# A two-layer attention trunk: hand-set order of the first stage, queued transposes, wider output chunks, last norm on VectorE

## Chip, core and metric

One NeuronCore of a Trainium2 chip runs the whole program in one launch. The metric is device time in microseconds (us), the median of several executions. PE is TensorE (PEld its weight loads), DVE is VectorE, ACT is ScalarE, POOL is GpSimd, and SP is the engine whose queue issues all DMAs here.

## What is computed

The input x is 512 tokens by 1024 features. Two layers follow each other, then one last RMSNorm. The four branches in a layer are latent attention (A), differential attention (B), top-k sparse attention (C) and a short convolution (D); each takes a slice of one input projection and is multiplied by a gate.

```
for l in range(2):
    h = rmsnorm(x, norm_g[l])
    p = split(h @ w_in[l])                 # 1024 -> 4040 columns
    o_a = mla(...); o_b = diff_attn(...); o_c = sparse(...); o_d = conv(...)
    y = concat([o_a * silu(gate_a), o_b * silu(gate_b), o_c * silu(gate_c), o_d * silu(gate_d)])
    x = x + y @ w_out[l]                   # 1024 x 1024
return rmsnorm(x, final_g)
```

## The kernel before

**Numbers.** Most products are made from float32 operands split into a high part and the rest, so that one product is three matmuls (`mm3`: high by high, high by rest, rest by high). A weight tile is loaded into a `wr` buffer (4 of them) and split by `split_w` (L103): ACT casts the high part `wh` (L106), POOL subtracts the rest `wl` in pieces of 256 columns (L101). `wh` and `wl` have 4 buffers each (`WB`).

**Order.** The program is written as streams that `merge` (L227) interleaves by estimated cost. A scheduler that works from a cost model then sets the order of each engine's queue. Inside `tc.manual_schedule(engines=...)` the engines named keep the order in which the program is written. Before the change only SP is named (`START`, L45), and only for the first stage of layer 0.

**First stage.** `FIRST[0]` (L30) is the list of its steps: `lT` loads token tile T of x (128 tokens), `wQ` loads a quarter Q of the first 456 weight columns, `sT` takes the squares and their sums on ACT (`Norm.part`), `nT` ends the norm (`Norm.finish`: Sqrt on ACT, five small DVE instructions, two DVE products with the norm weights g at L286), `eT` transposes the tile on PE (`Hidden.fill`, L302) and splits it (ACT cast L115, DVE subtraction L116), `cQ` splits a weight quarter (ACT cast, half of the subtraction on DVE at L108, half on POOL), and a pair of digits QT is the product of quarter Q with tile T (6 matmuls of 456 columns). After quarter 3 of a tile, `first_norm` (L521) works on that tile's result. `l0` also loads g, repeated to 128 rows, into a `wr` buffer (L245).

**Attention.** Six pairs of heads run per layer. A unit of a pair makes scores on PE, exponentials on ACT (L478) and normalised weights (L482). Two units later `turn` calls `flip` (L410), which transposes the 128x128 blocks of the weights on PE (L414), then casts (L115) and subtracts (L116). One unit later `prod` makes the product with the values (`ps_o`). 

**Output.** `out_first` (L859) multiplies the six parts of y that are ready early by w_out in four chunks of 256 columns: two weight tiles a chunk, four token tiles each, 18 matmuls per token tile. `LATE` (L47) puts the product of token tile 3 and chunk 3 off. `out_last` (L890) then adds the last two parts of y, 12 matmuls of 512 columns per token tile, and the matmuls put off. Each result is added to x on DVE (L888, L909) and handed to `after` (L1016), which makes the next norm: in layer 0 the squares, `finish` and, two token tiles later, the transposes of layer 1; in layer 1 the last norm, with `early` set: POOL multiplies by g in pieces of 256 columns (L272) while the squares are taken, and `finish` scales one half on DVE (L289) and one on ACT (L290).

Of the kernel before, what the change touches and what calls it, by code (L numbers as in the profile page):

```python
# [19 lines left out]
P = 128  # L20
# [9 lines left out]
FIRST = ("l0 w0 l1 l2 w1 l3 w2 w3 s0 n0 s1 c0 e0 00 n1 s2 c1 e1 01 10 11 n2 s3 e2 c2 02 12 20 21 n3 e3 c3 03 13 22 23 30 31 32 33",  # L30
# [14 lines left out]
START = {mybir.EngineType.SP}  # L45
FM = (456, 456)
LATE = ((3, 3),)  # L47
# [18 lines left out]
def hybrid_trunk(ctx, tc, x_in, norm_g, w_in, qa_g, w_uq, kva_g, w_ukv, dlam, subg,  # L66
# [55 lines left out]
    def mm3(o, terms, start=True, stop=True, skip=False):  # L122

        n = len(terms)
        for i, (ah, al, bh, bl) in enumerate(terms):
            for j, (a, b) in enumerate(((ah, bh), (ah, bl), (al, bh))):
                nc.tensor.matmul(o, lhsT=a, rhs=b, start=start and i == 0 and j == 0,  # L127
                                 stop=stop and i == n - 1 and j == 2, skip_group_check=skip)

# [118 lines left out]
    class Norm:  # L248


        def __init__(self, x, g, early=False):
            self.x, self.g, self.early = x, g, early
# [4 lines left out]
        def part(self, c):  # L257
            n, ss = self.n, self.ss
            self.n += 1
            jk = prob()  # L260
            nc.scalar.activation(jk[:, :c.stop - c.start], self.x[:, c], AF.Square, accum_out=ss[:, n:n + 1])
# [49 lines left out]
    def layer(l, hT, enter, after):  # L311
# [98 lines left out]
        def flip(p, qb, pts):  # L410
            nb = qb + 1
            b = bank("pt")
            for k in range(nb):
                nc.tensor.transpose(b[:, k * P:(k + 1) * P], p[:, k * P:(k + 1) * P], ident)  # L414
            c = (qb % 2) * P
            split_ps(pts[0][:, :nb, c:c + P], pts[1][:, :nb, c:c + P],
                     b[:, :nb * P].rearrange("p (k c) -> p k c", k=nb))
# [4 lines left out]
        def pair(k, unit, v, gt, post):  # L422

            yf = prob()
            for half in range(2):
                box = {}
                for j in range(2):
                    for qb in (2 * half, 2 * half + 1):
# [10 lines left out]
                        if qb % 2:  # L439
                            def prod(j=j, half=half, box=box):  # L440
# [4 lines left out]
                                pts = box[j]  # L445
                                for kb in range(nb):
# [3 lines left out]
                                        start=j == 0 and kb == 0, stop=j == 1 and kb == nb - 1, skip=True)  # L450
# [408 lines left out]
        def out_first():  # L859
# [7 lines left out]
            for n in range(4):  # L867
                c = slice(n * 256, (n + 1) * 256)
                ws = []
                for k0 in ((0, 3), (3, 6)):  # L870
                    raw = raw_tile()
                    rv = raw[:, :768].rearrange("p (k c) -> p k c", k=3)
                    if k0[0] == 0:
                        nc.sync.dma_start(rv, wo[:, 0:3, c])
                    else:
                        nc.sync.dma_start(rv[:, 0:1], wo[:, 3:4, c])
                        nc.sync.dma_start(rv[:, 1:3], wo[:, 6:8, c])
                    ws.append([w[:, :768].rearrange("p (k c) -> p k c", k=3) for w in split_w(raw, 768)])
                for t in range(NT):
                    ts_ = slice(t * P, (t + 1) * P)  # L880
                    terms = [(Y[k][:, 0, ts_], Y[k][:, 1, ts_], ws[i // 3][0][:, i % 3, :],
                              ws[i // 3][1][:, i % 3, :]) for i, k in enumerate(ks)]
# [4 lines left out]
                    yield from mm3g(o[:, :256], terms, 3, 0.33)  # L887
                    nc.vector.tensor_tensor(out=X[t][:, c], in0=o[:, :256], in1=X[t][:, c], op=OP.add)  # L888

        def out_last():  # L890
# [5 lines left out]
            for t in range(NT):  # L896
                ts_ = slice(t * P, (t + 1) * P)
                for n in range(2):
                    c = slice(n * 512, (n + 1) * 512)
                    o = bank("proj")  # L900
                    more = [m for m in (2 * n, 2 * n + 1) if (t, m) in put_off]
                    mm3(o, [(Y[4 + i][:, 0, ts_], Y[4 + i][:, 1, ts_], w[0][:, c], w[1][:, c])
                            for i, w in enumerate(ws)], stop=not more, skip=True)
                    for m in more:
                        mm3(o[:, (m % 2) * 256:(m % 2) * 256 + 256], put_off[t, m], start=False, stop=m == more[-1], skip=True)
# [85 lines left out]
    g0 = raw_tile()  # L991

    warm = sm.tile([P, 1], FT, name="warm", bufs=1)
    nc.scalar.activation(warm, ident[:, 0:1], AF.Sqrt)
# [99 lines left out]
```

## Time and profile before

| | us |
|---|---|
| median of 3 runs | 682.03 |
| lowest, highest | 677.0, 683.62 |
| profiled execution, its own time | 679.76 |
| its span in the trace | 678.0 |

The span is the time from the first to the last instruction on the core; 1.76 us of the execution lie outside it.

### The profile page before, as it was taken

To read this page: it belongs to the slowest core of one execution; us is meant where nothing else is said; L and a number is where in the kernel's file an instruction comes from. 1 tells how busy PE (TensorE), PEld (TensorE's weight loads), DVE (VectorE), ACT (ScalarE), POOL (GpSimd) and SP (SyncE) were. 2 spreads that over 40 slices of the span, in tenths; PEclk is the share of its full clock that TensorE was granted. 3 is DMA by queue.
4 is the path that set the end of the run, shared out by engine and by line. 5 is a ranking of instruction groups with operands and counts; after the bars stand their busy time and mean duration, and the time that the engine had idled before them with its cause. 6 is when DMAs were issued, how large, how long until landed. Compare 5 with 4: busy or idle time off the path is not lost.

```text
span 678.0 us, 11037 instructions
## 1 busy us (share of the span) xinstructions
PE 622.1 (92%) x3599; PEld 533.6 (79%) x3607; DVE 487.4 (72%) x1441; ACT 364.6 (54%) x879; POOL 278.5 (41%) x408
## 2 busy tenths in 40 slices
PE   1999999789999898999989899999999999999994
PEld 1877787678789677899968687879878977789994
DVE  3767762599999796645395767779999959664536
ACT  6556583484552564554364566866545256355435
POOL 2375432315434343442431854242534344344255
PEclk9999999799999999999999999999999999999998
DMA  8446573763455411233253653457244641132203
GB/s 262 117 111 191 148 133 94 185 158 99 109 145 151 118 47 43 83 125 114 58 169 91 181 171 103 139 135 170 65 115 116 190 117 48 47 109 100 80 1 125
DMA packets 86697, 80.71 MB, mean 119 GB/s; under 512 B 7302, under 2 KB 73400, under 8 KB 86640
## 3 DMA queue, kind: packets, MB, share of 16 engines
q1 hardware_dynamic: 86640, 80.02, 42.4%
q8 instruction: 28, 0.46, 0.3%
q14 instruction: 29, 0.24, 0.1%
HBM read 65.22 MB, written 12.16 MB: 114 GB/s over the span
## 4 chain that ended last, share of the span: by engine, by line
PE 58%; DVE 26%; ACT 7%; DMA 5%; issue 2%; POOL 1%; SPq 0%; ACTq 0%; DVEq 0%; POOLq 0%
PE ps_proj L127 43%; PE ps_o L127 5%; DVE ia L595 5%; DVE m L594 4%; PE ps_pt L414 3%; PE ps_s L127 2%; DMA wr<-in_w_in_dram 2%; DVE ptl L116 2%; DVE big L119 1%; DVE ps_s L490 1%; ACT prob L478 1%; DMA big<-in_x_dram 1%; PE ps_pt L302 1%; ACT prob L482 1%; DVE ia L581 1%
## 5 line engine op out<-in xcount | busy, mean ns | idle before, releaser
L101 POOL TENSOR_TENSOR wl<-wr,wh 128x256 fp32r<-128x256 f32 (+1 forms) x304 | 226.8, 779 | 326.1 <-ACT wh L106 279.4
L127 PE MATMUL ps_proj<-big,wh 128*128 128x512 f32 x768 | 250.7, 401 | 2.1 <-DVE prob L472 1.0
L127 PE MATMUL ps_proj<-wh,big 128*128 128x256 f32 (+2 forms) x768 | 173.1, 310 | 4.6 <-DVE big L116 2.1
L127 PEld LDWEIGHTS ps_proj<-big,wh 128*128 128x128 f32 x768 | 138.8, 189 | 26.8 <-issue 1.5
L127 PE MATMUL ps_proj<-big,wl 128*128 128x512 f32 x384 | 151.7, 395 | 0.0
L127 PEld LDWEIGHTS ps_proj<-wh,big 128*128 128x128 f32 x768 | 129.9, 193 | 9.6 <-DVE big L116 2.6
L127 PE MATMUL ps_proj<-wl,big 128*128 128x256 f32 (+2 forms) x384 | 116.8, 304 | 0.0
L106 ACT CAST wh<-wr 128x1024 fp32r<-128x1024 f32 (+2 forms) x84 | 83.8, 999 | 43.2 <-PE ps_proj L127 20.6
L127 PEld LDWEIGHTS ps_proj<-big,wl 128*128 128x128 f32 x384 | 72.3, 188 | 14.2
L127 PEld LDWEIGHTS ps_proj<-wl,big 128*128 128x128 f32 x384 | 74.4, 194 | 2.0
L116 DVE TENSOR_TENSOR ptl<-ps_pt,pth 128x128 fp32r<-128x128 f32 (+1 forms) x96 | 46.5, 485 | 31.4 <-ACT pth L115 30.8
L127 PE MATMUL ps_o<-pth,vt 128*128 128x256 f32 (+1 forms) x288 | 60.0, 280 | 5.2 <-ACT pth L115 3.9
L115 ACT CAST pth<-ps_pt 128x128 fp32r<-128x128 f32 (+1 forms) x96 | 40.5, 425 | 44.0 <-PE ps_pt L414 43.6
L478 ACT ACTIVATE prob<-ps_s,st_a 128x128 f32<-128x128 f32 (+1 forms) x64 | 33.8, 529 | 47.8 <-DVE st_a L490 30.7
L127 PEld LDWEIGHTS ps_o<-pth,vt 128*128 128x128 f32 x288 | 49.1, 194 | 10.0 <-ACT pth L115 6.5
L414 PE MATMUL ps_pt<-ident,prob 128*128 128x128 f32 x240 | 43.2, 278 | 10.2 <-ACT prob L482 7.1
L595 DVE MATCH_REPLACE8 ia<-m,ia 128x256 f32<-128x256 f32 (+2 forms) x96 | 52.0, 544 | 0.2
L594 DVE MAX8 m<-ia 128x8 f32<-128x256 f32 (+2 forms) x96 | 50.9, 550 | 0.1
L127 PE MATMUL ps_o<-ptl,vt 128*128 128x256 f32 (+1 forms) x144 | 42.3, 294 | 4.7 <-DVE ptl L116 4.7
L414 PEld LDWEIGHTS ps_pt<-ident,prob 128*128 128x128 f32 x240 | 28.5, 140 | 22.3 <-ACT prob L482 12.5
L482 ACT ACTIVATE prob<-prob,st_a 128x128 f32<-128x128 f32 (+1 forms) x64 | 35.8, 564 | 9.5 <-DVE st_a L481 9.3
L581 DVE SCALAR_TENSOR_TENSOR ia<-prob,widx,ia 128x256 f32<-128x256 f32 (+2 forms) x42 | 26.2, 639 | 12.7 <-ACT prob L576 12.0
(160 smaller groups left out, 949.1 us busy)
## 6 DMA issues: line engine op xcount, KB each, us to landing
wr<-in_w_in_dram SPq DMA_DIRECT2D x56, 512.0 KB
big<-trip SPq DMA_DIRECT2D x64, 128.0 KB
trip<-big SPq DMA_DIRECT2D x28, 256.0 KB
big<-in_x_dram SPq DMA_DIRECT2D x7, 512.0 KB
wr<-in_w_in_dram SPq DMA_DIRECT2D x8, 416.0 KB
big<-trip SPq DMA_DIRECT2D x32, 96.0 KB
wr<-in_w_out_dram SPq DMA_DIRECT2D x8, 384.0 KB
big<-big SPq DMA_DIRECT2D x8, 256.0 KB
```

Of the source, the lines that this page charges most:

```text
L101: nc.gpsimd.tensor_tensor(out=o[:, c], in0=a[:, c], in1=b[:, c], op=OP.subtract)
L106: nc.scalar.copy(h[:, :n], raw[:, :n])
L115: nc.scalar.copy(hi, src)
L116: nc.vector.tensor_tensor(out=lo, in0=src, in1=f(hi), op=OP.subtract)
L119: nc.vector.scalar_tensor_tensor(out=lo, in0=src, scalar=scale, in1=f(hi), op0=OP.mult, op1=OP.subtract)
L127: nc.tensor.matmul(o, lhsT=a, rhs=b, start=start and i == 0 and j == 0, stop=stop and i == n - 1 and j == 2, skip_group_check=skip)
L414: nc.tensor.transpose(b[:, k * P:(k + 1) * P], p[:, k * P:(k + 1) * P], ident)
L478: nc.scalar.activation(p[:, :W], s[:, :W], AF.Exp, scale=-1.0, bias=mn, accum_out=sums)
L482: nc.scalar.activation(p[:, :W], p[:, :W], AF.Copy, scale=st[:, 2:3])
L581: nc.vector.scalar_tensor_tensor(out=a, in0=r[:, :W], scalar=w, in1=a, op0=OP.mult, op1=OP.add)
L594: nc.vector.max(out=m8, in_=a)
L595: nc.vector.match_replace(out=a, in_to_replace=m8, in_values=a, imm_value=MARK)
```

## The change

Six things change.
1. START names ACT, DVE and PE beside SP, so in the first stage of layer 0 these keep the order of `FIRST[0]`, whose steps are rearranged.
2. g of layer 0 is loaded as one row of 4 KB and spread to 128 rows by two float32 matmuls with a row of ones (512 columns each), which ACT copies from PSUM. It no longer takes a `wr` buffer. The Sqrt that loads ACT's table is put ahead of the first squares.
3. `flip` no longer issues its transposes: it puts them in the list `riders`, and `mm3` issues one behind each of its matmuls; `prod` first issues all that are left.
4. `out_first` works in two chunks of 512 columns with three weight tiles each.
5. `LATE` is empty.
6. The last norm is made by `finish` on DVE (L286), as the others are.

```diff
-FIRST = ("l0 w0 l1 l2 w1 l3 w2 w3 s0 n0 s1 c0 e0 00 n1 s2 c1 e1 01 10 11 n2 s3 e2 c2 02 12 20 21 n3 e3 c3 03 13 22 23 30 31 32 33",
+FIRST = ("l0 w0 l1 w1 l2 w2 l3 w3 s0 n0 c0 e0 s1 00 n1 c1 e1 s2 10 01 11 n2 c2 e2 s3 20 21 02 12 22 n3 c3 e3 30 31 32 03 13 23 33",
...
-START = {mybir.EngineType.SP}
+START = {mybir.EngineType.SP, mybir.EngineType.Activation, mybir.EngineType.DVE, mybir.EngineType.PE}
...
-LATE = ((3, 3),)
+LATE = ()
...
-    def mm3(o, terms, start=True, stop=True, skip=False):
+    riders = []
+
+    def ride(n=1):
+
+        while riders and n:
+            riders.pop(0)()
+            n -= 1
+
+    def mm3(o, terms, start=True, stop=True, skip=False, carry=True):
...
                 nc.tensor.matmul(o, lhsT=a, rhs=b, start=start and i == 0 and j == 0,
                                  stop=stop and i == n - 1 and j == 2, skip_group_check=skip)
+                if carry:
+                    ride()
...
             jk = prob()
+            if self.warm and n == 0:
+
+                nc.scalar.activation(jk[:, 0:1], ident[:, 0:1], AF.Sqrt)
...
         def flip(p, qb, pts):
             nb = qb + 1
-            b = bank("pt")
+            c = (qb % 2) * P
+            box = []
+
+            def one(k):
+                if k == 0:
+                    box.append(bank("pt"))
+                b = box[0]
+                nc.tensor.transpose(b[:, k * P:(k + 1) * P], p[:, k * P:(k + 1) * P], ident)
+                if k == nb - 1:
+                    split_ps(pts[0][:, :nb, c:c + P], pts[1][:, :nb, c:c + P],
+                             b[:, :nb * P].rearrange("p (k c) -> p k c", k=nb))
+
             for k in range(nb):
...
+                riders.append(lambda k=k: one(k))
...
                                 pts = box[j]
+                                ride(99)
...
-            for n in range(4):
-                c = slice(n * 256, (n + 1) * 256)
+            for n in range(2):
+                c = slice(n * 512, (n + 1) * 512)
                 ws = []
-                for k0 in ((0, 3), (3, 6)):
+                for k0 in (0, 2, 6):
                     raw = raw_tile()
...
+                    nc.sync.dma_start(raw.rearrange("p (k c) -> p k c", k=2), wo[:, k0:k0 + 2, c])
+                    ws.append([w.rearrange("p (k c) -> p k c", k=2) for w in split_w(raw, 1024)])
...
-                    yield from mm3g(o[:, :256], terms, 3, 0.33)
-                    nc.vector.tensor_tensor(out=X[t][:, c], in0=o[:, :256], in1=X[t][:, c], op=OP.add)
+                    yield from mm3g(o, terms, 2, 0.65)
+                    nc.vector.tensor_tensor(out=X[t][:, c], in0=o, in1=X[t][:, c], op=OP.add)
...
-    g0 = raw_tile()
-
-    warm = sm.tile([P, 1], FT, name="warm", bufs=1)
-    nc.scalar.activation(warm, ident[:, 0:1], AF.Sqrt)
+    g0 = flat(big(FT))
+    grow = const.tile([1, D], FT, name="grow")
+    one = const.tile([1, P], FT, name="one")
+    nc.vector.memset(one, 1.0)
...
             if t == 0:
-                load_g(norm_g[0], g0)
-            x0[t] = Norm(x, g0)
+                nc.sync.dma_start(grow, norm_g[0:1, :])
+                for n in range(2):
+                    b = bank("pt")
+                    nc.tensor.matmul(b, lhsT=one, rhs=grow[:, n * 512:(n + 1) * 512], start=True, stop=True)
+                    nc.scalar.copy(g0[:, n * 512:(n + 1) * 512], b)
+            x0[t] = Norm(x, g0, warm=t == 0)
...
-                st["n"].append(Norm(x, st["g"], l + 1 == DEPTH))
+                st["n"].append(Norm(x, st["g"]))
```

## Rows read from the trace of the kernel before

**Rows 1.** The page, part 1 (busy us, share, instructions) and part 4 (chain).

```profile
PE 622.1 (92%) x3599; PEld 533.6 (79%) x3607; DVE 487.4 (72%) x1441; ACT 364.6 (54%) x879; POOL 278.5 (41%) x408
...
PE 58%; DVE 26%; ACT 7%; DMA 5%; issue 2%; POOL 1%; SPq 0%; ACTq 0%; DVEq 0%; POOLq 0%
```

**Rows 2.** Busy time by stretch: PE, PEld, DVE, ACT, POOL, granted clock, DMA.

```profile
0.00:13.80 13.80, 0.00 (x0) 0.00 (x0) 3.00 (x13) 7.98 (x17) 3.94 (x14) 1.00 0.78 257
...
290.00:334.60 44.60, 43.84 (x358) 42.59 (x359) 18.27 (x56) 20.52 (x45) 18.72 (x29) 1.00 0.32 103
...
348.10:352.00 3.90, 0.96 (x5) 0.58 (x4) 3.90 (x8) 1.37 (x4) 3.90 (x5) 1.00 0.64 146
353.00:357.00 4.00, 4.00 (x17) 3.38 (x16) 3.25 (x11) 2.75 (x8) 0.86 (x1) 0.57 0.70 218
```

**Rows 3.** Timeline of DVE, first 16 us: start, duration, idle before and releaser.

```profile
7.17 0.16 DVE L283 SCALAR_TENSOR_TENSOR nw<-nw 128x1 f32<-128x1 f32 x1
...
10.81 0.63 DVE L108 TENSOR_TENSOR wl<-wr,wh 128x456 fp32r<-128x456 f32 x1 [3.34 <-ACT wh L106]
...
12.94 1.41 DVE L286 SCALAR_TENSOR_TENSOR big<-big,nw,wr 128x512 f32<-128x512 f32 x2
...
14.94 0.42 DVE L116 TENSOR_TENSOR big<-ps_pt,big 128x256 fp32r<-128x256 f32 x1
```

**Rows 4.** Timeline of ACT, first 7 us.

```profile
3.49 0.63 ACT L261 ACTIVATE prob<-big 128x512 f32<-128x512 f32 x1 [1.48 <-DMA big<-in_x_dram]
...
4.96 1.28 ACT L278 ACT_TABLE_LOAD   x1
6.26 0.29 ACT L278 ACTIVATE nw<-ss 128x1 f32<-128x1 f32 x1
```

**Rows 5.** Groups by line, ACT: a copy of 512 columns from PSUM.

```profile
L841 ACT COPY prob<-ps_proj 128x512 f32<-128x512 f32 x4 | 2.3, 579 | 0.0
```

**Rows 6.** Timeline of PE, first 60 us.

```profile
13.84 1.09 PE L302 MATMUL ps_pt<-ident,big 128*128 128x128 f32 x4 [13.84 <-DVE big L286]
...
42.00 0.70 PE L127 MATMUL ps_proj<-big,wh 128*128 128x512 f32 x2 [0.79 <-DVE big L537]
...
44.93 0.66 PE L544 MATMUL ps_pt<-ident,prob 128*128 128x128 f32 x4 [0.85 <-DVE prob L621]
...
57.82 0.81 PE L215 MATMUL ps_pt<-prob,rb 32*12 32x384 f32 x2
```

**Rows 7.** The chain in order of time, first stage and output: start, length, what.

```profile
22.42 1.87 PE ps_proj L127 x9
...
299.36 1.08 PE ps_proj L127 x9
```

**Rows 8.** Timeline from 636 to 660: weight splits, and matmuls of 512 columns.

```profile
646.35 2.13 ACT L106 CAST wh<-wr 128x1024 fp32r<-128x1024 f32 x2 [1.84 <-PE ps_proj L127]
...
647.48 5.59 POOL L101 TENSOR_TENSOR wl<-wr,wh 128x256 fp32r<-128x256 f32 x8 [8.10 <-ACT wh L106]
...
656.86 0.39 PE L127 MATMUL ps_proj<-wl,big 128*128 128x512 f32 x1
...
657.54 0.39 PE L127 MATMUL ps_proj<-wl,big 128*128 128x512 f32 x1
```

**Rows 9.** Waits of PE: total us, times, longest.

```profile
PE ps_pt L414 <- ACT prob L482: 7.1, 10, 1.5
PE ps_o L127 <- DVE ptl L116: 4.7, 5, 1.5
PE ps_o L127 <- ACT pth L115: 3.9, 5, 1.7
```

**Rows 10.** Timeline of DVE, the last 10 us.

```profile
669.21 0.65 DVE L281 TENSOR_TENSOR nw<-nw 128x1 f32<-128x1 f32 x1
...
673.27 0.16 DVE L281 TENSOR_TENSOR nw<-nw 128x1 f32<-128x1 f32 x1
...
673.92 0.49 DVE L289 TENSOR_SCALAR big<-big,nw 128x512 f32<-128x512 f32 x1
```

More of the change, by code (lines that the diff above doesn't have):

```diff
@@ L248, in hybrid_trunk, with __init__ @@
     class Norm:
-        def __init__(self, x, g, early=False):
-            self.x, self.g, self.early = x, g, early
+        def __init__(self, x, g, early=False, warm=False):
+            self.x, self.g, self.early, self.warm = x, g, early, warm
             self.xn = flat(big(FT))
@@ L411, in flip @@
             nb = qb + 1
-            b = bank("pt")
+            c = (qb % 2) * P
[8 more added lines that the diff above has]
+                             b[:, :nb * P].rearrange("p (k c) -> p k c", k=nb))
             for k in range(nb):
[L414 to L417, printed above, removed]
+                riders.append(lambda k=k: one(k))
         late = []
@@ L449, in prod @@
                                                       + tuple(x[:, kb, c:256] for x in pts)],
-                                        start=j == 0 and kb == 0, stop=j == 1 and kb == nb - 1, skip=True)
+                                        start=j == 0 and kb == 0, stop=j == 1 and kb == nb - 1, skip=True, carry=False)
                                 return 0.33 * nb
@@ L866, in out_first @@
             wo = w_out[l].rearrange("(k p) c -> p k c", p=P)
-            for n in range(4):
-                c = slice(n * 256, (n + 1) * 256)
+            for n in range(2):
+                c = slice(n * 512, (n + 1) * 512)
                 ws = []
-                for k0 in ((0, 3), (3, 6)):
+                for k0 in (0, 2, 6):
                     raw = raw_tile()
[L872 to L878, printed above, removed]
+                    nc.sync.dma_start(raw.rearrange("p (k c) -> p k c", k=2), wo[:, k0:k0 + 2, c])
+                    ws.append([w.rearrange("p (k c) -> p k c", k=2) for w in split_w(raw, 1024)])
                 for t in range(NT):
                     ts_ = slice(t * P, (t + 1) * P)
-                    terms = [(Y[k][:, 0, ts_], Y[k][:, 1, ts_], ws[i // 3][0][:, i % 3, :],
-                              ws[i // 3][1][:, i % 3, :]) for i, k in enumerate(ks)]
+                    terms = [(Y[k][:, 0, ts_], Y[k][:, 1, ts_], ws[i // 2][0][:, i % 2, :],
+                              ws[i // 2][1][:, i % 2, :]) for i, k in enumerate(ks)]
                     if (t, n) in LATE:
@@ L900, in out_last @@
                     o = bank("proj")
[L901 to L905, printed above, removed]
+                    mm3(o, put_off.get((t, n), []) + [(Y[4 + i][:, 0, ts_], Y[4 + i][:, 1, ts_], w[0][:, c], w[1][:, c])
+                                                      for i, w in enumerate(ws)])
                     cuts = (0, 256, 512) if (l, t, n) == (DEPTH - 1, NT - 1, 1) else (0, 512)
```

## The prediction

> **What bounds the kernel now.** I read the busy times and the chain first [rows 1]. TensorE is busy 622 of 678 us and holds 58% of the chain, VectorE 26%. So a change pays if it takes work from TensorE or fills its idle time, and the question is where the other 56 us lie. Busy time by stretch answers that [rows 2]: the first 13.8 us hold no TensorE work at all; the output stage of layer 0 (290 to 334.6 us) is full, 43.84 of 44.60; behind it, at the step from layer 0 to layer 1, TensorE is busy 0.96 of 3.90 us while VectorE is busy throughout. The waits of TensorE [rows 9] give the rest: attention transposes wait for the normalised weights (7.1 us in 10 waits), value products for the split transposes (4.7 and 3.9 us in 5 waits each).
>
> In the first stage the timeline of VectorE shows that the late start is partly one of order. The norm factor of tile 0 is ready at 7.33 us [rows 3], but its products with g begin only at 12.94: in front of them stands a weight subtraction that waited 3.34 us for its cast [rows 3]. TensorE's first transpose follows at 13.84 [rows 6]. From there it works through the 96 first matmuls and 32 transposes until 41.2 us (42.00 less the 0.79 idle ahead of it [rows 6]); then come two idle spells of 0.79 and 0.85 us, for the norms of this stage [rows 6]. 41.2 is the mark that I compare with.
>
> **First stage: where the new order starts.** ACT now keeps the written order, and its first two instructions are the copies of g. I follow that chain. The first half of x has landed by 3.49 us [rows 4]; the 4 KB row of g is issued behind both halves, so I take 4.4 for it (estimate; 3.6 to 5.5). A float32 matmul of 384 columns took 0.81 us at full clock [rows 6]; two of 512 columns are 2 x 0.81 x 512/384 = 2.2 us, and more at the low clock: four transposes took 1.09 us at the start against 0.66 later [rows 6], a factor 1.65, so 3.6 us. The second matmul ends at about 7.9, its copy of 0.58 us [rows 5] at 8.5. The table load of 1.28 us [rows 4] then stands in front of the Sqrt: 9.8. Two squares at 0.73 us pitch (from 3.49 to 4.96 for both [rows 4]) end at 11.3, Sqrt and the small instructions take 1.07 (6.26 to 7.33 [rows 3, 4]), the first product with g half of 1.41 [rows 3]: 13.1. The first transpose comes at about 13.3, against 13.84. On SP's queue g's 512 KB go, and w0 to w3 move ahead of the x tiles; the DMA engines were 0.78 busy in this stretch [rows 2], so all these land sooner. But tile 0 waits for none of them, and behind the copies on ACT stand its squares, the Sqrt and the casts of the weights: nothing is won at the start.
>
> Whether the load stands behind the copies is a place where the Trainium skill (ScalarE activation tables, "Table sets in the compiler and the runtime") speaks: loads are placed for the greedy longest run. By that, with the copies counted to the run, one load could stand ahead of them, and the start would be 1.28 us earlier. This trace does not bear it out: there are two loads, one for the squares and one at 4.96 directly ahead of the Sqrt, though both functions run later without a load between them, so a run was not looked for there. The sum does not use it.
>
> **First stage: how long it runs.** Every engine now takes tiles in turn, and s1 stands on ACT behind all four casts of e0. From one tile's first transpose to the next: four groups of transposes share two PSUM banks, so the third group waits for cast and subtraction of the first (14.94 + 0.42 against 13.84, 1.5 us a round [rows 3, 6]): 2.7 us in all to the last cast (estimate); then squares 1.46, Sqrt and small ones 1.07, product 0.70, hand-over 0.2: 6.1, rounded up to 6.5 for in-order waits. TensorE has less than that to do in the first two gaps: 8 transposes and 6 matmuls, then 8 and 18, at 0.15 (0.66/4 [rows 6]) and 0.208 us (1.87/9 [rows 7]): 2.4 and 4.9 us. First transposes thus at 13.3, 19.8 and 26.3. Behind tile 2 stand 30 matmuls, 6.2 us, that TensorE must pass before tile 3's transposes: 26.3 + 2.7 + 6.2 = 35.2. Then 2.7 and the last 42 matmuls, 8.7: the stage ends at 46.7, against 41.2, +5.5. Tiles 0 to 2 then have their first_norm behind them, so the two spells of 0.79 and 0.85 go: -1.6. I take **+4**. The lower bound is +2, with the table load early (-1.3) and g at 3.6 (-0.8). The upper bound is +9: at half clock the 18 and the first of the 30 matmuls double (+3.7 and +1.5).
>
> **Output chunks and LATE.** A matmul of 256 columns costs 0.120 us (9 in 1.08 [rows 7]), one of 512 columns 0.227 (three in 0.68, 656.86 to 657.54 [rows 8]); the fixed share of 0.013 is paid half as often. A layer had 288 of the first, 34.6 us, and has 144 of the second, 32.6: -1.9. But LATE held 18 of the 288, 2.2 us, in a place where TensorE waits anyway: 0.96 busy of 3.90 [rows 2], VectorE and the norms set the pace there. These 2.2 us move in front of out_last, which therefore starts 0.25 us later. Then the buffers: a chunk now holds three of four wh/wl pairs, not two. The next chunk's second tile can be split only when its buffer is given back, six matmuls into the last token tile. A cast takes 1.06 and four POOL pieces 2.8 us (2.13 for two casts, 5.59 for eight pieces [rows 8]), so the second tile is ready 4.0, the third 6.8 us after that; TensorE comes to the third after 24 matmuls, 5.4 us, plus the attention between them. The last weight tile of out_last meets the same thing and POOL's last split of y. I put 0.75 us a layer for both (0 to 2.2). Together +1 a layer, **+2**; bounds -3.8 (the lost cover costs nothing) and +5. The bytes of the weights, and the pieces on POOL, stay the same in number.
>
> **Last norm on VectorE.** It removes 16 POOL pieces and four ACT scalings and makes VectorE's half product of 0.49 [rows 10] two of 1.41 together [rows 3]: 4 x 0.92 = +3.7 us of VectorE. Against that, small instructions that took 0.65 beside POOL and 0.16 without it [rows 10] lose 0.49 each; six did so, -2.9. VectorE paces this stretch: **+0.5** (-1.5 to +2).
>
> **Queued transposes.** The number of transposes stays, and so does their price; each now stands behind one matmul of another group. A wait for the weights shrinks by at most one matmul, 0.23, in 10 waits: -2.3. The split transposes come up to three matmuls later, which lengthens waits of value products if the scheduler doesn't make up for it (5 + 5 waits). I take **-2**; bounds -7.1 (all waits on weights go) and +4 (half of 10 x 0.7).
>
> **Sum.** +4 +2 +0.5 -2 = +4.5 on the profiled execution: 679.76 to 684.3. That execution lies 2.3 us below the median, which would give 686.5. I forecast **686**. A measurement of this kernel tells 1%, 675.2 to 688.9, from no change.
>
> **Rivals.**
> - *Faster: the queue of transposes takes most of the waits.* Transposes behind matmuls find their weights ready (-7 of the 7.1) and value products a little (-2 of 8.6), the chunk loses only matmul overhead without stalls (-3), the first stage +3, the tail 0: 682 - 9 = 673. For it: the waits are there, and a matmul in front of each fills part of it. Against it: one matmul is 0.23 us long and the mean wait is 0.7.
> - *Slower: the clock falls in the first stage.* At the step between the layers TensorE was busy 0.96 of 3.90 us and the granted clock was then 0.57 for 4 us [rows 2], that is, mostly the lower level. In the new first stage it has 7.3 us of work in the 13 us between tile 0 and tile 2. If the clock stays at 1.2 GHz there, the stage costs +9; with full weight stalls (+4 in the chunks) this gives 682 + 9 + 4 + 0.5 - 2 = 694. It decides from the point where the gaps between two tiles' transposes outlast TensorE's work in them, 13.3 to 26 us by the chain above. The Trainium skill (TensorE: Matmul & The Clock Gate, "Part 1: The HAM clock gate") says the same: the slow clock is the resting state and activity releases it; it speaks against an order with gaps.
> - *The order changes little.* If the scheduler's order for ACT, VectorE and TensorE was near the written one, or others' work fills the gaps, the stage gives 0 and the sum is 682.5.
>
> **How the numbers follow.** Forecast 686, own range 680 to 693, chance 0.40. Faster rival 673: 0.25. Slower rival 694: 0.20. Little change 682.5: 0.15. Faster by over 1% (below 675.2): nearly all of the 673 case, 0.24. Slower by over 1% (above 688.9): the 694 case and a third of the forecast's, 0.32. The rest, 0.44, lies within 1%. The range, 672 to 697, leaves out about 0.1 at each end.
>
> **What the profile after would show.** Right: TensorE's first transposes of tiles 0 to 3 near 13, 20, 26 and 35 us, the end of the 96 matmuls near 47, casts waiting for transposes on ACT; a gap of TensorE before the third weight tile of the second output chunk; an idle stretch at the step between the layers about 2 us longer; no POOL in the last 10 us, with a VectorE that is busy to the end; less waiting of the transposes for the weights. Wrong: a dense TensorE from 10 us on (then the first-stage chain is mis-read), waits on weights that are gone altogether, or a granted clock below 1 through the first 40 us.

## The result, and the profile after

The changed kernel takes 686.71 us (median of 10 runs, 683.31 to 688.8) against 681.93 for the kernel before in the same session (10 runs, 677.0 to 685.61): ratio 1.0083, interval [1.0059, 1.0107], so some 5.7 us slower. The forecast was 686 and "within 1%". Its profiled execution took 687.75 us, span 685.9, 7.9 more than the span before. The prediction's total came out; the rest of this document is about its four terms, two of which had the wrong sign.

Parts 1 and 4 of the page after, beside [rows 1]:

```profile
PE 629.7 (92%) x3323; PEld 522.2 (76%) x3323; DVE 484.5 (71%) x1432; ACT 361.0 (53%) x873; POOL 268.5 (39%) x392
...
PE 57%; DVE 24%; ACT 7%; issue 6%; POOL 3%; DMA 2%; SPq 0%; DVEq 0%; ACTq 0%; POOLq 0%
```

TensorE is busy 7.6 us longer with 276 instructions fewer; 3.75 of that are the new broadcast of g. That is the first thing to see: the loss is not idle time alone, matmuls themselves took longer. The timeline of TensorE in the first 50 us (start, duration, group, idle time before and its releaser), beside [rows 6]:

```profile
3.85 3.75 PE L1027 MATMUL ps_pt<-grow,one 1*128 1x512 f32 x4 [3.85 <-DMA grow<-in_norm_g_dram]
13.14 2.16 PE L315 MATMUL ps_pt<-ident,big 128*128 128x128 f32 x8 [5.54 <-DVE big L299]
...
18.89 0.65 PE L315 MATMUL ps_pt<-ident,big 128*128 128x128 f32 x4 [1.31 <-DVE big L299]
...
26.15 1.03 PE L315 MATMUL ps_pt<-ident,big 128*128 128x128 f32 x8
...
33.22 1.03 PE L315 MATMUL ps_pt<-ident,big 128*128 128x128 f32 x8
...
43.03 0.73 PE L135 MATMUL ps_proj<-big,wh 128*128 128x512 f32 x2
...
47.23 0.63 PE L566 MATMUL ps_pt<-ident,prob 128*128 128x128 f32 x4 [1.84 <-DVE prob L643]
```

The first stage begins at 13.14 (13.84 before) and its 96 matmuls are done at 43.0 (41.2 before): 1.8 us late. From 26.15 to 43 us it is dense, and the eight transposes of a tile run together, in 1.03 us. Then stands one wait of 1.84 us, where the kernel before had two of 0.79 and 0.85. ACT at the start, beside [rows 4]:

```profile
0.73 1.28 ACT L1028 ACT_TABLE_LOAD   x1 [0.73 <-PEq L1099]
...
7.64 0.59 ACT L1028 COPY big<-ps_pt 128x512 f32<-128x512 f32 x1 [1.12 <-PE ps_pt L1027]
8.24 1.28 ACT L273 ACT_TABLE_LOAD   x1
```

Busy time by stretch (us; PE, PEld, DVE, ACT, POOL, then granted clock, DMA share, GB/s), beside [rows 2]:

```profile
13.10:43.00 29.90, 27.97 (x129) 24.00 (x129) 23.95 (x65) 18.35 (x56) 10.84 (x12) 0.94 0.29 76
...
127.00:133.00 6.00, 5.87 (x27) 5.88 (x28) 1.10 (x3) 0.00 (x0) 1.31 (x4) 0.50 0.84 238
144.00:147.00 3.00, 3.00 (x13) 2.71 (x12) 1.95 (x5) 2.95 (x8) 1.41 (x2) 0.50 0.03 5
...
185.00:188.00 3.00, 3.00 (x10) 2.22 (x9) 2.02 (x9) 0.67 (x2) 0.49 (x1) 0.50 0.72 182
297.00:342.00 45.00, 45.00 (x238) 36.77 (x237) 17.16 (x48) 20.02 (x44) 14.68 (x24) 1.00 0.20 61
353.70:358.70 5.00, 0.78 (x5) 0.56 (x4) 5.00 (x13) 3.47 (x9) 3.00 (x4) 1.00 0.51 167
359.00:365.00 6.00, 5.39 (x17) 4.61 (x18) 4.27 (x14) 1.49 (x4) 0.00 (x0) 0.50 0.68 175
```

The granted clock is at its lower level (0.50, that is 1.2 GHz) in five stretches while TensorE has work: inside the first stage, then at 127 to 133, 144 to 147, 185 to 188 and 359 to 365. The trace of before shows it in two, around 121 to 128 and 353 to 357 (the second lies in [rows 2]). Which stretches fall differs from one execution of a kernel to the next: the mean granted clock of the ten executions lies between 0.978 and 0.986, and the traced one, with 0.978, is at the low end. The output stage, in which I expected stalls, is full: 45.00 of 45.00. The step between the layers (353.7 to 358.7) holds 0.78 us of TensorE work; in its timeline the idle time before the first matmul of layer 1 is

```profile
358.06 0.47 PE L135 MATMUL ps_proj<-wh,big 128*128 128x456 f32 x1 [4.22 <-ACT big L115]
...
359.61 0.75 PE L135 MATMUL ps_proj<-wh,big 128*128 128x456 f32 x1 [0.66 <-DVE big L116]
```

4.22 + 0.66 = 4.9 us, where before it was 3.90 - 0.96 = 2.9 [rows 2]. The waits of TensorE (total us, times, longest), beside [rows 9]:

```profile
PE ps_pt L432 <- ACT prob L504: 5.6, 7, 1.7
PE ps_o L135 <- ACT pth L115: 4.8, 5, 1.7
...
PE ps_o L135 <- DVE ptl L116: 3.3, 6, 1.3
PE ps_proj L135 <- DVE prob L792: 2.0, 1, 2.0
```

The three named waits add up to 13.7 us, 15.7 before. And the end, on VectorE, beside [rows 10]:

```profile
667.35 0.69 DVE L923 TENSOR_TENSOR big<-ps_proj,big 128x512 f32<-128x512 f32 x1 [0.67 <-PE ps_proj L135]
...
672.23 0.16 DVE L294 TENSOR_TENSOR nw<-nw 128x1 f32<-128x1 f32 x1
...
681.35 1.41 DVE L299 SCALAR_TENSOR_TENSOR big<-big,nw 128x512 f32<-128x512 f32 x2
```

From the first result of out_last to the end of VectorE's work it is 15.4 us (667.35 to 682.76); before, 657.52 to 674.41, 16.9. The small instructions take 0.16 all the way.

### The profile page after: what moved, and what is told of

The parts are those of the page before. It is cut to its first block, busy times and chain, and to the rows that moved or that the text cites. A ratio compares the mean times of both kernels' runs of the same rounds, so it can differ in the third digit from the quotient of the medians.

```text
span 685.9 us, 10393 instructions
## 1 busy us (share of the span) xinstructions
PE 629.7 (92%) x3323; PEld 522.2 (76%) x3323; DVE 484.5 (71%) x1432; ACT 361.0 (53%) x873; POOL 268.5 (39%) x392
## 4 chain that ended last, share of the span: by engine, by line
PE 57%; DVE 24%; ACT 7%; issue 6%; POOL 3%; DMA 2%; SPq 0%; DVEq 0%; ACTq 0%; POOLq 0%
PE ps_proj L135 41%; PE ps_o L135 5%; DVE ia L617 4%; DVE m L616 3%; PE ps_pt L432 3%; PE ps_s L135 2%; POOL wl L101 2%; DVE big L299 2%; DVE ptl L116 2%; ACT prob L500 1%; ACT wh L106 1%; DVE big L119 1%; DVE ia L603 1%; PE ps_pt L315 1%; DVE ps_s L512 1%
## 5 line engine op out<-in xcount | busy, mean ns | idle before, releaser
L135 PE MATMUL ps_proj<-big,wh 128*128 128x512 f32 x768 | 257.1, 407 | 4.2 <-DVE prob L792 2.0
L135 PE MATMUL ps_proj<-wh,big 128*128 128x512 f32 (+2 forms) x576 | 166.8, 364 | 5.7 <-ACT big L115 4.2
L135 PEld LDWEIGHTS ps_proj<-big,wh 128*128 128x128 f32 x768 | 140.8, 190 | 33.5 <-DVE prob L792 2.2
L135 PE MATMUL ps_proj<-big,wl 128*128 128x512 f32 x384 | 154.6, 403 | 0.0
L135 PEld LDWEIGHTS ps_proj<-wh,big 128*128 128x128 f32 x576 | 105.4, 197 | 18.2 <-ACT big L115 4.6
L135 PE MATMUL ps_proj<-wl,big 128*128 128x512 f32 (+2 forms) x288 | 104.5, 363 | 0.1
L106 ACT CAST wh<-wr 128x1024 fp32r<-128x1024 f32 (+1 forms) x80 | 83.1, 1039 | 34.4 <-PE ps_proj L135 13.7
L432 PE MATMUL ps_pt<-ident,prob 128*128 128x128 f32 x240 | 59.7, 278 | 10.1 <-ACT prob L504 5.6
L135 PEld LDWEIGHTS ps_proj<-wl,big 128*128 128x128 f32 x288 | 56.8, 197 | 6.5 <-DVE wl L108 0.4
L432 PEld LDWEIGHTS ps_pt<-ident,prob 128*128 128x128 f32 x240 | 32.5, 142 | 19.2 <-ACT prob L504 10.6
L135 PE MATMUL ps_o<-ptl,vt 128*128 128x256 f32 (+1 forms) x144 | 42.8, 297 | 3.3 <-DVE ptl L116 3.3
```

The source lines that it names most:

```text
L106: nc.scalar.copy(h[:, :n], raw[:, :n])
```

## Experiments

Twelve kernels, each with its ratio to the kernel before of the same session; 0.001 is 0.68 us. An interval is about 0.002 to either side, so two ratios that lie 0.003 (2 us) apart are just told apart.

**1. The changed kernel with one part put back.** Four kernels; the diffs are the change's own reversed, cut to their first lines. The old first stage (with it the old list of steps, load of g and early Sqrt):

```diff
-START = {mybir.EngineType.SP, mybir.EngineType.Activation, mybir.EngineType.DVE, mybir.EngineType.PE}
+START = {mybir.EngineType.SP}
...
-                nc.sync.dma_start(grow, norm_g[0:1, :])
+                load_g(norm_g[0], g0)
```

> The changed kernel with its first stage put back (old list of steps, only SP in the written order, g loaded to 128 rows, Sqrt warmed at the very start); the other five parts stay. Three theories, against 686.7 us of the changed kernel. The prediction's own term (the first stage costs +4): 682.7. The two traces read as they stand, the loss being only what TensorE is late at the end of the stage (42.9 against 41.2 us): -1.7, 685.0. The third: the lag of 5.8 us that the changed kernel has at about 160 us is all an echo of the new first stage: 681.

Measured 1.0049 [1.0029, 1.0070], so the new first stage costs 0.0034, 2.3 us. The later end of the stage explains 1.8 of it, the longer wait behind it 0.2 (1.84 against 0.79 + 0.85); what is left is within the uncertainty. The echo theory (5.8 us) falls. The prediction's +4 is not excluded by the time alone; the two marks in the trace, 2.0 us together, speak against it.

Transposes at once:

```diff
-                riders.append(lambda k=k: one(k))
+                nc.tensor.transpose(b[:, k * P:(k + 1) * P], p[:, k * P:(k + 1) * P], ident)
```

> The changed kernel with the attention transposes issued at once, as a block, instead of queued behind matmuls; the other parts stay. The prediction's term (the queue gains 2): 688.7. The rival, that the lag which grows by 3 to 4 us between 45 and 160 us is made by the queue (split transposes come later, value products wait longer): 683. A third, that the waits only change their names: 686.7 within 1.

Measured 1.0044 [1.0025, 1.0063]: the queue costs 0.0039, 2.7 us, where I had put a gain of 2. The three named waits add up to 15.5 us here (6.0, 5.6, 3.9), 13.7 with the queue, so the queue does shorten them. Yet the same 3323 TensorE instructions are busy 3.1 us less without it (626.6 us against 629.7). Part of that is seen in the stretches; first the changed kernel, with the row of TensorE behind which the clock falls, then this one:

```profile
185.00:188.00 3.00, 3.00 (x10) 2.22 (x9) 2.02 (x9) 0.67 (x2) 0.49 (x1) 0.50 0.72 182
```
```profile
184.29 0.82 PE L135 MATMUL ps_proj<-big,wh 128*128 128x512 f32 x2 [1.97 <-DVE prob L792]
```
```profile
177.00:184.00 7.00, 7.00 (x33) 5.50 (x33) 7.00 (x24) 4.06 (x11) 5.62 (x8) 1.00 0.30 75
```

At 184.29 a projection matmul, which reads the hidden state and a weight tile, waits 1.97 us for VectorE's normalised weights (L792), and the clock falls behind it. The transposes of these weights hang in its group, behind the seventh matmul. Without the queue TensorE is busy all of 7.00 us in the same place, at 1.00. This is no chance of one execution: all seven kernels here with the queue show the clock at 0.50 between 180 and 190 us, six of them behind this very wait of 1.97 or 1.98 us (the seventh, where all transposes ride at once, behind one of 1.47), and the seven without it 1.00 from 160 to 197. The fall at 144 to 147 is there in three of the seven. The one at 21 to 24, which this kernel does not have either, lies in the first stage, the same code in both, and is none of the queue's; it is there in four of the seven kernels with that stage.

But the fall at 184 is not where the queue's time goes. Two marks enclose it, a cast on ACT and a product on VectorE; first the changed kernel, then this one:

```profile
168.37 0.61 ACT L418 CAST big<-prob 128x512 fp32r<-128x512 f32 x1
231.35 0.41 DVE L827 TENSOR_TENSOR prob<-prob,ps_pt 128x256 f32<-128x256 f32 x1
```
```profile
165.36 0.61 ACT L418 CAST big<-prob 128x512 fp32r<-128x512 f32 x1
229.32 0.41 DVE L819 TENSOR_TENSOR prob<-prob,ps_pt 128x256 f32<-128x256 f32 x1
```

From one to the other it is 63.0 us with the wait and the fall, and 64.0 without. The changed kernel is 3.0 us behind at the first mark and 2.0 at the second; all seven kernels with the queue take 63.0 to 63.1 us from mark to mark, the five that have neither queue nor useless work 63.9 to 64.0. The distance grows earlier: it is 0.3 at 107 us (the tanh of a gate, 107.60 against 107.30), and the fall at 144 makes up some 0.7 of the growth in this trace. Nor is the mean granted clock lower with the queue: 0.978 to 0.986 in the executions of either kernel. What makes up the rest of the 2.7 us is not shown.

The four chunks of 256 columns, two weight tiles each, and the product put off:

```diff
-LATE = ()
+LATE = ((3, 3),)
...
-            for n in range(2):
-                c = slice(n * 512, (n + 1) * 512)
+            for n in range(4):
+                c = slice(n * 256, (n + 1) * 256)
```

> The changed kernel with the output in four chunks of 256 columns and the product of token tile 3 with the last chunk put off again; the other parts stay. The prediction's term (+2 for both layers): 684.7. The two traces read stretch by stretch (+1.3 before out_last in layer 0, +1.0 at the step between the layers, about +1 in the output of layer 1): 683.4, with the idle time of TensorE at the step back at about 3 us from 4.9. The rival, that these are later echoes of the lag at 285 us and the wide chunks gain their matmul overhead (2 us a layer less): 688 or more.

Measured 1.0044 [1.0021, 1.0067]: wide chunks with nothing put off cost 0.0039, 2.7 us. The theory that reads the traces stretch by stretch had 3.3 us, the prediction's term 2; this measurement does not tell them apart, and excludes the rival alone, by which the wide chunks gain.

The old last norm:

```diff
-                st["n"].append(Norm(x, st["g"]))
+                st["n"].append(Norm(x, st["g"], l + 1 == DEPTH))
```

> The changed kernel with the last norm multiplied by g on POOL and scaled half on DVE, half on ACT, as before; the other parts stay. The prediction's term (the norm on DVE costs +0.5): 686.2. The traces (from the first to the last DVE instruction of the last output stage 15.4 us against 16.9): the norm on DVE gains 1.5, so 688.2, with DVE's instructions of 128x1 back at 0.65 us beside POOL from 0.16.

Measured 1.0119 [1.0090, 1.0148]: the norm on VectorE gains 0.0036, 2.5 us (give or take as much); the prediction had +0.5. With POOL back, the end of VectorE's timeline reads

```profile
676.99 0.85 DVE L302 TENSOR_SCALAR big<-big,nw 128x512 f32<-128x512 f32 x1
...
678.61 0.65 DVE L294 TENSOR_TENSOR nw<-nw 128x1 f32<-128x1 f32 x1
```

The four parts undone give 2.3 + 2.7 + 2.7 - 2.5 = 5.2 of the 5.7 us: they nearly add, and no large part of the loss lies between them, as far as differences known to some 2 us each can say.

**2. What the queue costs.** All queued transposes behind the first matmul that comes by:

```diff
                 if carry:
-                    ride()
+                    ride(99)
```

> The changed kernel, in which the first matmul that comes by takes all queued transposes behind it, not one each; all else stays. The theory that the spreading costs (a part of a group waits behind others' matmuls, the split transposes come later): as with the transposes at once, 2 to 3 less, ratio 1.004 to 1.005, and no stretch of lower clock near 144 and 185 us. The rival that the place in the queue costs, behind a matmul of another group instead of in front: no gain, ratio 1.008, with these stretches still there.

Measured 1.0081 [1.0050, 1.0112]: no gain is seen. That speaks for the rival, by which to stand behind a matmul of another group costs as much as the spreading, though the interval reaches the 1.005 of the first theory. The second theory's detail came only in part: the stretch near 185 us is there, and longer, but 144 to 147 is at 1.00.

```profile
180.00:186.00 6.00, 4.57 (x15) 3.59 (x15) 5.74 (x23) 2.18 (x6) 4.24 (x7) 0.50 0.44 101
```

**3. The step between the layers.** First 18 matmuls that nobody reads, in the idle stretch, in layer 0 alone:

```diff
+            if l == 0:
+                o = bank("proj")
+                for i in range(18):
+                    nc.tensor.matmul(o, lhsT=Y[4][:, 0, 0:P], rhs=ws[0][0][:, 0:512], start=i == 0, stop=i == 17)
```

> The changed kernel with 18 matmuls of 512 columns behind out_last of layer 0 whose result nobody reads (18 x 0.227 = 4.1 us): they move no work, they only keep TensorE running in the idle stretch of 4.9 us at the step. The theory that the lower clock behind that stretch costs: the granted clock from 358.9 to 365.7 us, 0.50 in the changed kernel, is 1.00, and 1.5 to 3 us are won, ratio 1.004 to 1.006. The rival that TensorE is paced there by the norms on VectorE: the clock is 1.00, and nothing is won, ratio 1.008. A third, that the useless matmuls stand in the way of the transposes: a loss of up to 2, ratio 1.011.

The stretches and the timeline of TensorE:

```profile
355.00:360.00 5.00, 5.00 (x26) 4.09 (x24) 5.00 (x14) 3.65 (x9) 1.78 (x2) 1.00 0.51 181
360.30:367.00 6.70, 5.79 (x32) 4.96 (x32) 5.39 (x15) 2.10 (x7) 1.34 (x2) 1.00 0.69 180
```
```profile
354.89 0.39 PE L135 MATMUL ps_proj<-wh,big 128*128 128x512 f32 x1
355.12 4.24 PE L928 MATMUL ps_proj<-wh,big 128*128 128x512 f32 x18
...
387.02 0.63 PE L566 MATMUL ps_pt<-ident,prob 128*128 128x128 f32 x4 [1.40 <-DVE ssa L554]
```

The clock is 1.00 behind it. From the last matmul of out_last to the fixed mark at L566 it is 32.1 us (354.89 to 387.02); in the changed kernel 35.0 (353.45 to 388.44):

```profile
388.44 0.63 PE L566 MATMUL ps_pt<-ident,prob 128*128 128x128 f32 x4 [1.39 <-DVE ssa L554]
```

So 2.9 us are won at this place with work that computes nothing. The clock is not the only thing that changed there. From the first transposes of layer 1 to the first cast of their result on ACT it is 5.5 us (351.95 to 357.47), in the changed kernel 7.2 (350.47 to 357.65): the cast now stands ahead of the last tile's Sqrt, not behind it. That makes up 1.7 of the 2.9; the 1.2 behind the cast go with the matmuls at full clock. Of the whole time less is left: 1.0065 [1.0041, 1.0088], 0.0018 or 1.2 us, which this measurement alone does not tell from none.

Then real work in the same place: the third weight tile's share of two token tiles is put off to out_last (12 matmuls, 2.7 us a layer).

```diff
-LATE = ()
+LATE = ((2, 1), (3, 1))
...
                     if (t, n) in LATE:
-                        put_off[t, n] = terms
-                        continue
+                        put_off[t, n] = terms[4:]
+                        terms = terms[:4]
```

> The changed kernel, in which the third weight tile's share of token tiles 2 and 3 with the second chunk (6 matmuls of 512 columns each, 12 in all, 12 x 0.227 = 2.7 us a layer) is put off to out_last; all else stays. The theory that the lost cover is the cost: at the step between the layers TensorE's idle stretch goes from 4.9 to about 2.2 us and the lower clock behind it shortens; 2.7 in layer 0, 0.5 to 1 for the clock, 0 to 1 in the tail: -3 to -4, ratio to the kernel before 1.003 to 1.004. The prediction's size (0.25 us a layer for the later start): -0.5, ratio 1.0075. The rival that VectorE paces the step and the tail alike, so that the work moved comes late for token tiles 2 and 3: 0 or a loss, ratio 1.008 or more.

Measured 1.0046 [1.0024, 1.0067], 2.5 us below the changed kernel. Its trace shows L566 at 381.33, 7.1 earlier than the changed kernel (2.7 of that it had before the output stage, where the stretches at 21 to 24 and at 144 to 147 us are at 1.00 in this execution), and TensorE nearly dense and at full clock through the step:

```profile
349.70:354.70 5.00, 3.83 (x17) 2.65 (x16) 4.12 (x11) 4.47 (x10) 1.98 (x2) 1.00 0.26 105
355.00:361.00 6.00, 5.98 (x32) 4.95 (x33) 5.96 (x16) 3.05 (x9) 3.31 (x4) 1.00 0.76 225
```

In layer 1 some of it is given back: VectorE takes the first result of out_last 8.8 us earlier than the changed kernel (658.56 against 667.35), the last only 5.8 (672.56 against 678.32). So the next kernels put off in layer 0 alone.

**4. The kernel before with parts of the change.** The norm on VectorE alone:

```diff
-                st["n"].append(Norm(x, st["g"], l + 1 == DEPTH))
+                st["n"].append(Norm(x, st["g"]))
```

> The kernel before with one part alone of the change: the last norm on VectorE, no work on POOL or ACT for it. The prediction's term: +0.5, ratio 1.001. What the traces and the undoing of this part say (1.5 to 2.5 us of the tail won): ratio 0.9965 to 0.998. The rival that POOL's help is only worth as little in the changed kernel because the tail there has no product put off: no gain, ratio 1.000 or above.

Measured 0.9978 [0.9951, 1.0005]: 1.5 us won, of the sign that undoing it showed, though the interval just holds 1. The norm, the wide chunks of the change, and the put-off work of experiment 3 in layer 0:

```diff
-LATE = ((3, 3),)
+LATE = ((2, 1), (3, 1))
...
-                    if (t, n) in LATE:
-                        put_off[t, n] = terms
-                        continue
+                    if l == 0 and (t, n) in LATE:
+                        put_off[t, n] = terms[4:]
+                        terms = terms[:4]
```

> The kernel before with the last norm on VectorE, two output chunks of 512 columns, and, in layer 0 alone, the third weight tile's share of token tiles 2 and 3 with the second chunk put off to out_last (2.7 us of matmuls into the idle stretch at the step between the layers); old first stage, transposes at once. The theory of lost cover and lower clock: the norm gains 1.5, the wide chunks cost 2.7 in the changed kernel, of which the put-off work takes back 4.4 at the step: 1.5 + 1.7 = 3.2 us below the kernel before, ratio 0.995. The rival that the narrow chunks of the kernel before fill the step as well (2.2 us put off): 1.5 below, ratio 0.998.

Measured 0.9937 [0.9917, 0.9957], median 675.49 us against 679.99: faster than both kernels by 4.3 and some 10 us. And the same without the put-off work:

```diff
-LATE = ((2, 1), (3, 1))
+LATE = ()
```

> The kernel before with the last norm on VectorE and two output chunks of 512 columns, nothing put off; it differs from the kernel with work put off in layer 0 (ratio 0.9937) in that alone. The theory of lost cover: the idle stretch of TensorE at the step between the layers is back at 4 to 5 us with a stretch of lower clock behind it, 4.4 us lost: ratio 1.000. The rival that the wide chunks gain by themselves in the old schedule (36.6 matmuls' worth of fixed cost, 1.9 us a layer) and that the put-off work is worth only its own 2.7: ratio 0.9977 or below. The third, that what is won comes from a stretch of lower clock which happens to fall elsewhere: ratio 0.994 still.

Measured 1.0002 [0.9978, 1.0027]. The two differ only in where these 12 matmuls stand, 2.7 us of work, and by 0.0065, 4.4 us, of time, as the theory of lost cover had it. The first transposes of layer 1, the first cast of their result on ACT and the mark at L544 (L566 in the changed kernel), with the put-off work and without:

```profile
343.81 0.60 PE L302 MATMUL ps_pt<-ident,big 128*128 128x128 f32 x4
...
348.38 0.36 ACT L115 CAST big<-ps_pt 128x256 fp32r<-128x256 f32 x1
...
377.22 0.63 PE L544 MATMUL ps_pt<-ident,prob 128*128 128x128 f32 x4 [1.41 <-DVE ssa L532]
```
```profile
343.64 0.60 PE L302 MATMUL ps_pt<-ident,big 128*128 128x128 f32 x4
...
350.83 0.63 ACT L115 CAST big<-ps_pt 128x256 fp32r<-128x256 f32 x2
...
381.60 0.63 PE L544 MATMUL ps_pt<-ident,prob 128*128 128x128 f32 x4 [1.40 <-DVE ssa L532]
```

33.4 us with it, 38.0 without: 4.6 us lie in the step. 2.6 of them pass ahead of the first cast, which stands ahead of the last tile's last square on ACT with the put-off work and behind it without; no run tells this order from the cover itself. 1.9 pass behind the cast, where the clock is 0.50 from 352.2 to 358.7 without the put-off work and 1.00 with it. That the clock differs is no chance of two executions: its mean is 0.988 to 0.992 in the six with the put-off work, 0.977 to 0.987 in the twelve without.

The last kernel also gives three of the terms a second time, since each of three others differs from it in one part: the first of experiment 1 in the queue (1.0049 against 1.0002, 3.2 us), the second in the first stage (1.0044, 2.9 us), and the first of this experiment in the chunks and the product put off (0.9978, 1.6 us). All three have the sign that the undoing gave.

**5. The lower clock elsewhere.** The kernel before has such a stretch at 121 to 128 us, behind waits of 1.74 and 1.05 us. On top of the norm, 14 matmuls that nobody reads in front of the last value product of the first pair:

```diff
+        def idle(n):
+            b = bank("pt")
+            for i in range(n):
+                nc.tensor.matmul(b, lhsT=hT.k(0)[0][:, 0:P], rhs=hT.k(1)[0], start=i == 0, stop=i == n - 1)
...
                                 pts = box[j]
+                                if (l, k, j, half) == (0, 0, 1, 1):
+                                    idle(14)
```

> The kernel before with the last norm on VectorE, and 14 matmuls of 512 columns that nobody reads (14 x 0.227 = 3.2 us) in front of the last value product of the first pair of heads, where TensorE of the kernel before waits 1.74 and, one matmul later, 1.05 us (121.96 and 123.58 us) and the granted clock is 0.50 from 121.3 to 128.1 us. The theory that the lower clock has a price wherever TensorE has work behind an idle stretch: that stretch of 0.50 goes or becomes shorter, and 1.5 to 2.5 us are won on top of the norm's 1.5, ratio 0.9945. The rival that the weights of the next pair arrive late there anyway: the clock is 1.00 and nothing more is won, ratio 0.998. A third, that useless work delays the value product: ratio 1.000.

Measured 0.9995 [0.9977, 1.0013], no gain over 0.9978. The stretches of this kernel, and then of the one without the useless work:

```profile
122.00:128.00 6.00, 5.93 (x43) 5.39 (x42) 2.79 (x5) 0.70 (x2) 3.12 (x5) 1.00 0.57 186
198.00:201.00 3.00, 3.00 (x16) 3.00 (x16) 2.89 (x12) 0.00 (x0) 0.88 (x2) 0.50 0.91 287
225.30:228.30 3.00, 3.00 (x10) 2.42 (x9) 2.21 (x8) 1.34 (x4) 0.00 (x0) 0.50 0.77 224
```
```profile
122.00:128.00 6.00, 4.40 (x19) 4.11 (x20) 3.05 (x5) 1.00 (x3) 3.36 (x5) 0.50 0.50 166
198.00:201.00 3.00, 1.68 (x15) 1.60 (x14) 3.00 (x11) 1.74 (x3) 2.06 (x3) 1.00 0.62 220
225.30:228.30 3.00, 2.41 (x13) 2.06 (x13) 2.29 (x12) 2.00 (x6) 0.00 (x0) 1.00 1.05 295
```

The clock was held where it was meant to be, and the scores of the second pair came 2.2 us earlier (the first exponential on ACT at 132.43 against 134.61). But then it fell at 198 and at 225, where it had not, and a mark at 230 us (a subtraction on VectorE at 229.92 against 229.63) was 0.3 late. The fall at 198 is in the two kernels with this useless work and in none of the others. It has a price: between the two marks of experiment 1 that enclose it these two take 65.3 and 65.4 us, 1.4 more than the kernels without. The one at 225 is also in the two kernels of experiment 4 with wide chunks, which have none, so the useless work need not be its cause. That edit on top of the kernel with the ratio 0.9937:

```diff
                                 pts = box[j]
+                                if (l, k, j, half) == (0, 0, 1, 1):
+                                    idle(14)
```

> Both of the last two together: the last norm on VectorE, two output chunks with work put off in layer 0, and 14 useless matmuls in front of the last value product of the first pair. If the parts add: 1.5 + 1.7 + 2 = 5.2 us below the kernel before, ratio 0.992. If the clock falls again elsewhere, in the next idle stretch, for what was won in one: no better than the better of the two, 0.995.

Measured 0.9940 [0.9921, 0.9959]: no better than without the useless work at 121 us (0.9937). The parts do not add here: in its trace the stretch of lower clock at 123 to 127 us is gone, but another stands at 138 to 144 (0.50), and the fall at 198 is there again.

## Why the prediction was right, and where it was not

The total, 686.0 against 686.7, is right by luck: two terms with the wrong sign cancel. In the order of the prediction, with the measured size (from undoing each part) behind its term: first stage +4, 2.3; output chunks and LATE +2, 2.7; last norm +0.5, -2.5 (-1.5 on the kernel before); queued transposes -2, +2.7. The sum of the terms was +4.5, that of the measured ones +5.2.

**First stage, where it starts: right.** The chain held link by link: row of g at 3.85 (4.4), broadcast 3.75 us (3.6), second copy done at 8.23 (8.5), table load to 9.52 (9.8), first transpose 13.14 (13.3). The Trainium skill (ScalarE activation tables, "Table sets in the compiler and the runtime") says loads go to the greedy longest run. This trace has one load at 0.73, ahead of the copies, and still a second of 1.28 us at 8.24 directly ahead of the Sqrt; measured, the copies' load did not serve the Sqrt, and the sum rightly left the rule out.

**First stage, how long it runs: mis-sized.** The failing step is that "four groups of transposes share two PSUM banks, so the third group waits for cast and subtraction of the first", 2.7 us, and that the matmuls behind tiles 2 and 3 are added to it. The eight transposes at 26.15 and 33.22 ran in 1.03 us without such a wait, and the next matmuls, which belong to earlier tiles, began at 26.94 and 34.01, 0.8 us behind them: twice 1.9 us less, which is the miss of the end (43.0 against 46.7). The tiles came at 18.9, 26.2 and 33.2, not 19.8, 26.3 and 35.2, and the end was 1.8 late, not 5.5. (0.66/4 is 0.165 us a transpose, not 0.15; that moves no mark.) The other half of the term failed in the opposite direction: "the two spells of 0.79 and 0.85 go: -1.6". They became one of 1.84: the small instructions of the last first_norm now run beside POOL's weight pieces, ahead of the copy that TensorE waits for. VectorE there:

```profile
44.63 0.76 DVE L555 TENSOR_TENSOR ssa<-ssa 128x2 f32<-128x2 f32 x1
...
46.05 0.69 DVE L556 SCALAR_TENSOR_TENSOR ssa<-ssa 128x2 f32<-128x2 f32 x1
```

With the one between them (0.82 at 45.31, 0.22 before) they take 1.7 us more. The same two lines took 0.16 in the kernel before from 42.8 to 44.4 us, where POOL was idle, and 0.66 at 39.65 and 0.70 at 45.91, where it was not. The Trainium skill (SBUF — State Buffer, "Who interferes with whom") says that a VectorE instruction with two SBUF inputs contends with a GpSimd instruction that reads SBUF; these rows, and that of 0.65 at 678.61 in experiment 1, agree.

**Output chunks and LATE: the sum near, its parts wrong.** I put 0.75 us a layer for stalls before late weight tiles and 0.25 for the lost cover. The stalls, and the gap that I named as their sign, are not there (45.00 of 45.00 in layer 0). The cover is worth more than 0.25: the idle stretch grew from 2.9 to 4.9 us, and the stretch of lower clock behind it is twice as long. Experiment 4 (0.9937 against 1.0002) shows that 2.7 us of work put off there are worth 4.4; how much of it is the cover, and how much the other order of ACT, stays open.

**Last norm: mis-sized.** I set 3.7 us of longer products against six small instructions at 0.49 each. Beside POOL the scaling of half a tile is slower too (0.85 at 676.99 against 0.49 [rows 10]), and in the kernel with the old norm seven small instructions are slow, not six. In its tail, to the end of the last norm on ACT, VectorE is busy 14.2 of 17.0 us, in that of the changed kernel 13.1 of 15.4: 1.0 less, not 0.8 more. The rest of the 1.6 are waits that went, which I did not count; by the traces of the kernel before with and without this part it is 0.7 in all.

**Queued transposes: the step failed that equates a shorter wait with a shorter time.** The named waits fell by 2.0 us (15.7 to 13.7), the size I had put, those for the weights by 1.5 of it. I asked who waits for the transposes, and not who stands behind them: a wait for the weights now holds a group of projection matmuls (1.97 us at 184.29), and the clock falls behind it. Yet that wait and that fall are not the price, since nothing of them is left at 231 us. The time grew by 2.7 us (3.2 in the second comparison), in the traces above all between 107 and 165 us; by which mechanism stays open. Experiment 2 speaks against the spreading. The bound of +4 held the measured 2.7.

**The rivals.** The slower one named a mechanism that was there and did not set the time: the clock did fall in the first stage (0.94 from 13 to 43 us), but in the kernel of the second reversal, with the same first stage and 1.00 from 20 to 24, the tiles came at most 0.8 us earlier and the end 0.2. (The two differ less than the column says: there the matmuls stand 0.38 us apart until 22 us.) At the step between the layers the lower clock went with 1.2 to 1.9 us; behind the wait at 184 us no loss was left. The faster one fell with the queue; that the order changes little (0 for the first stage) is further from the measured 2.3 than its +4. Of the signs I had named, the idle stretch at the step 2 us longer, no POOL in the last 10 us and shorter waits for the weights came; tiles at 20, 26 and 35 us and an end near 47 came only in part, and the gap in the output stage did not come. Of the signs of being wrong, a granted clock below 1 came, but from 21 to 24 us alone.

## What to carry to other kernels

Look first whether an engine's busy time grew with the same instructions; if so, read the granted clock stretch by stretch before any wait. But take the price of a slow stretch from marks on both sides of it: the one at 184 us cost nothing by 231. Work put off into an idle stretch of TensorE can be worth more than its own length (2.7 us here, worth 4.4), so it must not be taken out for a saving of instruction overhead without a measurement. A term that is right in total can hide two that are wrong: undo the parts one at a time.

## What was not expected of the hardware

Holding the clock in one place went with a fall in another: with useless work at 121 us it was 1.00 there and 0.50 at 198, where the same instructions ran at 1.00 in every kernel without that work, and the 2.2 us won were gone by 230 us. At the step between the layers useless work won 2.9 us (1.2 of them behind the first cast, and 1.2 of the whole time, not clear of none), and 2.7 us of real work 4.4. Between the same two marks the fall at 198 went with 1.4 us more, the wait and the fall at 184 with none. So a stretch of lower clock that a trace shows is not a fixed price of its place. And at the start of the program the column does not show the pace: it reads 1.00 there, while the eight transposes at 13.14 took 2.16 us, against 1.03 at 26.15, and matmuls of 456 columns stood 0.38 us apart until 17 us, against 0.21 from 24.5 on.
